# The second feed-forward product with its operands turned round

## The chip, the cores and the metric

One core of one Trainium2 chip. The metric is the device time of one execution in microseconds (us), taken as the median of several runs. Times inside an execution come from one profiled execution and count from the first instruction.

## The reference

One layer of a transformer-like trunk on 512 tokens of width 2048, all in float32: a normalised and modulated input goes through two groups of mixing heads and an output projection (with a residual sum), and then through a gated feed-forward block. The change touches the last product of the last line only:

```python
h = rms_norm(x, norm2_g[layer]) * (1.0 + sc2) + sh2
gate, up = jnp.split(h @ w_ffn_in[layer], 2, axis=-1)
x = x + g2 * ((jax.nn.silu(gate) * up) @ w_ffn_out[layer])
```

The hidden width is 5632 (44 blocks of 128). The output leaves the kernel transposed, as 16 blocks of 128 features by 512 tokens.

## The kernel before, in words

**Three passes.** TensorE multiplies numbers of the type float32r. Each float32 operand is split into a rounded part (`hi`, a ScalarE copy, line 231) and the rest (`lo`, a VectorE subtraction, line 232), and a product is summed from three passes: hi by hi, hi by lo, lo by hi. In all matmuls one operand is stationary (loaded as a block of 128x128) and the other one moves through it; the profile shows the load as PEld and the pass as PE.

**Seven products for eight.** Both feed-forward products are cut into halves in both directions and done with seven block products instead of eight, numbered 1 to 7; sums and differences of the blocks are operands. In the first feed-forward product (lines 1145 to 1191, tiles ffA, ffB, ffC) the loop runs over 42 blocks `f` of hidden features. There the weight block is stationary, and 256 tokens of the activation operands opA to opD move: 7 products of 24 matmuls of 128x256 a block. Two hidden blocks were done before, chunk by chunk, into tiles named ff (lines 985 to 1008), in the same orientation.

**The second product.** Its loop (lines 1267 to 1334) runs over 12 units: six chunks of hidden features (3, 3, 4, 4, 4, 4 steps of 128 of the half width 22), and in each two groups `i` of output columns. A unit does the seven products in the order 2, 1, 7, 6, 4, 5, 3. `multiply` (line 1217) does one product, in pieces of two steps (or one): it splits a 128 x 2 x 512 piece of the weights, then for each of two blocks of 128 tokens takes the activations as the stationary operand and 512 weight columns as the moving one. The accumulators are `A` (two banks, foA), `B` (two for each `i`, foB) and `C` (foC). After a product ScalarE copies the accumulators out (`onto`, line 1239) or VectorE adds them to `O`, which holds tokens in the partitions and 2048 features in the row. The activation operands come by DMA into places in opsA, opsB and opsC.

**The end.** In the two units of the last chunk (units 10 and 11) parts of `O` become final. As the output is wanted with features in the partitions, `emit_out` (line 1252) transposes two 128x128 blocks on TensorE (line 98, with the identity `ident2` stationary) into a half bank that belonged to foB, VectorE multiplies by the gate `G2` and adds the residual (line 1259), and SyncE sends 128x256 numbers out (line 1261). `some_out(3)` puts at most three of those behind each product; what is left comes behind the last one.

**Where the split weights lie.** `ring_pair` (line 211) takes a tile of 2048 + 128 numbers from a ring of three and puts hi and lo at `home[0]` and `home[0] + 1024`; every fourth split goes to a spare place (`spare_here`, later `spare_there`, line 1197). `home[0]` is 48 numbers in the first feed-forward product, with one exception: it is 0 in product 3 of every sixth block (`f % 6 == 4`, line 1178), and it is 0 in all of the second product (line 1202). In the built program before, ring tiles and all moving operands start 32 bytes past a multiple of 256 within a partition, so that the stationary and the moving start differ by 192 bytes modulo 256 with `home[0]` 48, and by 0 with `home[0]` 0. I call that the offset of a pair.

**Order.** A scheduler orders each engine's queue by priorities; splits and copies out carry a raised priority (`AHEAD`).

Of the kernel before, what the change touches and what calls it, by code (L numbers as in the profile page):

```python
# [10 lines left out]
F32 = mybir.dt.float32  # L11
F32R = mybir.dt.float32r
# [5 lines left out]
P = 128  # L18
D = 2048
# [110 lines left out]
def trunk(ctx, tc, a):  # L130
# [79 lines left out]

    def ring_pair(shape, name):
        n = int(np.prod(shape[1:]))
        t = wp.tile([P, 2048 + 128], F32R, tag="pair", name=name)
        out = []
        for b in (home[0], home[0] + 1024):
            v = t[:, b:b + n]
            if len(shape) == 3:
                v = v.rearrange("p (a b) -> p a b", a=shape[1])
            elif len(shape) == 4:
                v = v.rearrange("p (a b c) -> p a b c", a=shape[1], b=shape[2])  # L220
            out.append(v)
        return out
# [42 lines left out]


    hhi = hp.tile([P, KT, T], F32R, tag="hhi", name="hhi")
    hlo = hp.tile([P, KT, T], F32R, tag="hlo", name="hlo")
    xo = xop.tile([P, KT, T], F32, tag="xo", name="xo")
    vctx = ctx.enter_context(ExitStack())  # L270
    vp = vctx.enter_context(tc.tile_pool(name="vp", bufs=1))
# [531 lines left out]


    ohi = hp.tile([P, KT, T], F32R, tag="hhi", name="ohi")
    olo = hp.tile([P, KT, T], F32R, tag="hlo", name="olo")
    last = NH - 1

    def split_o(k):
# [198 lines left out]
                hold(0)  # L1008

    late = hp.tile([P, 2, HALF, 2, HT], F32R, tag="hhi", name="opB")  # L1010
    later = hp.tile([P, 2, HALF, 2, HT], F32R, tag="hlo", name="opC")
    H.update({6: late[:, 0], 7: late[:, 1], 5: later[:, 0], 4: later[:, 1]})
    for j in range(0, HALF, 2):
        V.tensor_sub(block(0, 0, j, 2), block(0, 1, j, 2), block(0, 0, j, 2))
# [55 lines left out]

    yraw = []

    def begin_second():
# [10 lines left out]
        places.append(hp.tile([P, 4, 4, 2, HT], F32R, tag="hlo", name="opsB"))  # L1084
# [107 lines left out]
    tctx.close()  # L1192


    more = places[1][:, 3].rearrange("p n h t -> p (n h t)")

    def spare_there(shape, name):
        n = shape[1] * shape[2]
        return [more[:, i * 1024:i * 1024 + n].rearrange("p (k d) -> p k d", k=shape[1]) for i in range(2)]

    spare[0] = spare_there
    home[0] = 0


    zp = ctx.enter_context(tc.tile_pool(name="zp", bufs=1, side="right", reuse_waits="tile"))
    T2 = []
    ident2 = zp.tile([P, 512], F32, name="ident2")[:, 0:P]
    O = zp.tile([P, 4, D], F32, name="O")
# [8 lines left out]
    def multiply(out, c, q, raw, first, u, sums):  # L1217
        n = CHUNKS[c]
        x = place(7 * c + q)
        for k0 in range(0, n, 2):  # L1220
            w = min(2, n - k0)
            with tc.high_priority(offset=AHEAD):
                for d, e, g in sums:
                    with tc.issue_after(mark[0 if q == 3 and k0 == 0 else 1]):
                        V.tensor_sub(*(t[:, k0:k0 + w] for t in (d, e, g)))
            whi, wlo = split(raw[:, k0:k0 + w], [P, w, T], f"wfo{u}_{q}_{k0}")
            if q == 2:
                mark[k0 > 0] = last_lo[0]
            for j in range(2):
                js = slice(j * P, j * P + P)  # L1230
                for kk in range(w):
                    k = k0 + kk
                    flags = dict(stop=False, skip_group_check=True)
                    PE.matmul(out[j], x[:, k, 0, js], whi[:, kk], start=first and k == 0, **flags)
                    PE.matmul(out[j], x[:, k, 0, js], wlo[:, kk], start=False, **flags)
                    flags["stop"] = k == n - 1
                    PE.matmul(out[j], x[:, k, 1, js], whi[:, kk], start=False, **flags)

    def onto(dst, src, first):
        if first:  # L1240
            with tc.high_priority(offset=2 * AHEAD):
                S.copy(dst, src)
            return
        t = cond[:, taps[0] % 4 * T:taps[0] % 4 * T + T]
        taps[0] += 1
        with tc.high_priority(offset=2 * AHEAD):
            S.copy(t, src)
        V.tensor_add(dst, dst, t)

    slots, turn, outs = [], [0], []  # L1250

    def emit_out(m, th):
        ps = slots[turn[0] % len(slots)]
        turn[0] += 1
        src = O[:, 2 * th:2 * th + 2, m * P:m * P + P]
        for j in range(2):
            PE.transpose(ps[:, j * P:j * P + P], src[:, j], ident2)
        xr = place(7 * (last_c + 1) + m // 4).bitcast(F32).rearrange("p n h t -> p n (h t)")[:, m % 4, th * HT:th * HT + HT]
        V.scalar_tensor_tensor(src, ps.rearrange("p (j t) -> p j t", j=2), mcol(G2, m),
                               xr.rearrange("p (j t) -> p j t", j=2), op0=ALU.mult, op1=ALU.add)  # L1260
        nc.sync.dma_start(a["y"][m][:, th * HT:th * HT + HT].rearrange("p (j t) -> p j t", j=2), src)

    def some_out(n):
        for _ in range(min(n, len(outs))):
# [1 line left out]

    for u, (c, i) in enumerate(units):
        def dst(th, j, dh):
            return O[:, 2 * th + j, dh * 1024 + i * T:dh * 1024 + i * T + T]
# [9 lines left out]
        if u == 2:  # L1279
            nc.sync.dma_start(ident2, a["cst"][:, 0])  # L1280
        y = blocks[u]
        if u == 1:
            T2.append(rp.tile([P, 4, T], F32, tag="forms", name="T2", bufs=1))
        s7 = (T2[0] if u else yraw[0][:, 2])[:, 0:CHUNKS[c]]
        load_y(u + 1, 2)
        load_y(u + 1, 0)
        for q, p in enumerate(ORDER):
            out = {2: B[i], 7: C, 4: C}.get(p, A)
            raw = {2: y[2], 1: y[0], 7: s7, 6: y[1], 4: y[2], 5: y[0], 3: y[3]}[p]
            sums = {6: [(y[0], y[1], y[0]), (y[1], y[3], y[0])], 4: [(y[2], y[2], y[1])]}.get(p, ())  # L1290
            if p == 7:
                with tc.high_priority(offset=AHEAD):
                    for k0 in range(0, CHUNKS[c], 2):
                        ks = slice(k0, min(k0 + 2, CHUNKS[c]))
                        V.tensor_sub(s7[:, ks], y[3][:, ks], y[1][:, ks])
            multiply(out, c, q, raw, p in (1, 7) or p == 2 and first, u, sums)
            if final:
                some_out(3)
            for j in range(2):
                if p == 1:  # L1300
                    onto(dst(0, j, 0), A[j], first)
                    if final:
                        V.tensor_add(dst(0, j, 0), B[i][j], dst(0, j, 0))
                elif p == 7:
                    onto(dst(1, j, 1), C[j], first)
                elif p == 6:
                    onto(dst(1, j, 0), A[j], first)
                elif p == 4:
                    V.tensor_add(dst(1, j, 0), C[j], dst(1, j, 0))
                elif p == 5:  # L1310
                    onto(dst(1, j, 1), A[j], False)
                elif p == 3:
                    if first:
                        S.copy(dst(0, j, 1), A[j])
                    else:
                        V.tensor_add(dst(0, j, 1), A[j], dst(0, j, 1))
            if p == 1:
                ready(0, 0)
                if final:
                    slots += [t[:, h * HT:h * HT + HT] for t in B[i] for h in range(2)]  # L1320
# [12 lines left out]
            if i == 1 and 1 <= q < 4:  # L1333
                load_op(c + 1, q + 3)
# [60 lines left out]
```

## Time and profile before

| | us |
|---|---|
| median of 3 runs | 2238.33 (2236.74 to 2240.53) |
| the profiled execution, its own time | 2237.67 |
| its span, first to last instruction | 2235.9 |
| TensorE matmuls busy | 2203.0 |
| VectorE busy | 1918.1 |
| ScalarE busy | 1160.9 |
| start of the second product (first foB) | 1801.8 |
| first transposition behind the last foA matmul | 2227.35 |

The profiled time exceeds its span by 1.8 us, which lie outside the instructions. A row of the timeline has the start, the length of a run of equal instructions, the engine, the line, output and inputs, the tile's shape and the count; in brackets stands the idle time before it and what ended it. The length of a run of matmuls includes the modelled end of the last one, so a pace is read from start to start.

### The profile page before, as it was taken

The page shows a single profiled execution, that of the slowest core. Times are in us where ns is not written, and L with a number is a line of the kernel's source. Part 1 is how long each engine was busy: PE and PEld are TensorE (multiplying, and loading weights), DVE is VectorE, ACT ScalarE, POOL GpSimd, SP SyncE. Part 2 cuts the span into 40 slices and gives each one's busy share as a digit, 9 for nine tenths or more (in the row PEclk, how much of TensorE's full clock was granted, in tenths as well). Part 3 has the DMA queues.
Part 4 walks back from the last instruction along what each step waited for, and adds up shares of the span by engine and source line. Part 5 has one row for each costly group of instructions (what it writes and reads, how often), then busy time and mean ns, then how long its engine had stood idle before and what let it go on. Part 6 is the DMA issues. An engine that isn't in the chain of part 4 may idle for free.

```text
span 2235.9 us, 35417 instructions
## 1 busy us (share of the span) xinstructions
PE 2203.0 (99%) x14171; PEld 2010.8 (90%) x14171; DVE 1918.1 (86%) x2500; ACT 1160.9 (52%) x1986; POOL 10.1 (0%) x25
## 2 busy tenths in 40 slices
PE   7999999999999999999999999999999999999999
PEld 6899899988888888899999999999999988888887
DVE  8897878899988877698888888888888888988888
ACT  4326665566565632385555555555555555545453
POOL 0000000000000000000000000000000000000000
PEclk9999999999999999999999999999999999999999
DMA  9886536754333288724444444444454486666452
GB/s 369 314 328 243 185 133 225 298 197 153 136 113 113 86 304 337 251 96 170 156 170 156 162 164 144 171 143 169 138 176 147 163 336 251 245 224 234 146 214 68
DMA packets 115264, 437.68 MB, mean 196 GB/s; under 512 B 9854, under 2 KB 58268, under 8 KB 77340
## 3 DMA queue, kind: packets, MB, share of 16 engines
q1 hardware_dynamic: 115100, 435.42, 54.0%
q8 instruction: 111, 1.82, 0.3%
q14 instruction: 53, 0.43, 0.1%
HBM read 386.61 MB, written 48.77 MB: 195 GB/s over the span
## 4 chain that ended last, share of the span: by engine, by line
PE 87%; DVE 8%; ACT 2%; DMA 2%; issue 2%; SPq 0%; DVEq 0%; ACTq 0%
PE ffA L93 20%; PE foA L93 11%; PE ffC L93 10%; PE wo L93 7%; PE foC L93 5%; PE ffB L93 5%; PE sbp L93 4%; PE st L93 4%; PE hgf L93 4%; PE hgg L93 4%; PE hgq L93 4%; PE foB L93 3%; PE ff L93 2%; DVE ada L179 2%; DVE wsb L232 1%
## 5 line engine op out<-in xcount | busy, mean ns | idle before, releaser
L93 PE MATMUL sbp<-wsb,hhi 128*128 128x384 f32 x1024 | 270.1, 343 | 3.0 <-DVE wsb L232 1.8
L179 DVE SCALAR_TENSOR_TENSOR ada<-ada,cond 128x2048 f32<-128x2048 f32 x95 | 217.0, 2287 | 20.3 <-DMA ada<-in_w_ada 20.1
L93 PEld LDWEIGHTS sbp<-wsb,hhi 128*128 128x128 f32 x1024 | 184.2, 189 | 7.5 <-issue 3.3
L93 PE MATMUL sbp<-wsb,hlo 128*128 128x384 f32 x512 | 172.4, 337 | 0.0
L93 PE MATMUL wo<-ohi,wo 128*128 128x512 f32 x480 | 149.3, 391 | 1.3 <-ACT ohi L810 1.3
L93 PEld LDWEIGHTS wo<-ohi,wo 128*128 128x128 f32 x480 | 89.9, 188 | 19.7 <-ACT ohi L810 1.5
L231 ACT CAST wfo<-wfo 128x1024 fp32r<-128x1024 f32 (+1 forms) x72 | 72.6, 1008 | 57.6 <-PE foA L93 51.8
L232 DVE TENSOR_TENSOR wfo<-wfo,wfo 128x1024 fp32r<-128x1024 f32 (+1 forms) x72 | 83.4, 1162 | 20.8 <-ACT wfo L231 20.2
L93 PEld LDWEIGHTS sbp<-wsb,hlo 128*128 128x128 f32 x512 | 96.6, 189 | 0.8 <-issue 0.5
L93 PE MATMUL ffA<-opB,ff 128*128 128x256 f32 x768 | 92.8, 276 | 1.0 <-ACT ff L231 1.0
L93 PE MATMUL ffA<-opD,ff 128*128 128x256 f32 x768 | 93.6, 278 | 0.0
L93 PE MATMUL wo<-olo,wo 128*128 128x512 f32 x240 | 93.4, 390 | 0.0
L93 PE MATMUL ffC<-opC,ff 128*128 128x256 f32 x768 | 92.5, 276 | 0.0
L93 PE MATMUL ffB<-opA,ff 128*128 128x256 f32 x768 | 92.4, 276 | 0.0
L93 PEld LDWEIGHTS ffA<-opB,ff 128*128 128x128 f32 x768 | 89.8, 188 | 1.2 <-ACT ff L231 1.2
L93 PEld LDWEIGHTS ffA<-opD,ff 128*128 128x128 f32 x768 | 90.7, 189 | 0.0
L93 PE MATMUL ffA<-opC,ff 128*128 128x256 f32 x744 | 89.7, 276 | 0.0
L93 PEld LDWEIGHTS ffC<-opC,ff 128*128 128x128 f32 x768 | 89.6, 188 | 0.0
L93 PE MATMUL ffC<-opB,ff 128*128 128x256 f32 x744 | 89.6, 276 | 0.0
L93 PEld LDWEIGHTS ffB<-opA,ff 128*128 128x128 f32 x768 | 89.5, 188 | 0.0
L93 PE MATMUL ffA<-opA,ff 128*128 128x256 f32 x744 | 89.5, 276 | 0.0
L93 PE MATMUL st<-wi,hhi 128*128 128x512 f32 x256 | 75.8, 397 | 11.7 <-ACT hhi L317 11.7
(1003 smaller groups left out, 5884.3 us busy)
## 6 DMA issues: line engine op xcount, KB each, us to landing
ada<-in_w_ada SPq DMA_DIRECT2D x95, 1024.0 KB, 6.4
wfo<-in_w_fo SPq DMA_DIRECT2D x16, 1024.0 KB, 5.0
yraw<-in_w_fo SPq DMA_DIRECT2D x16, 1024.0 KB, 4.9
fix<-in_w_fix SPq DMA_DIRECT2D x14, 1024.0 KB, 5.2
opd<-forms SPq DMA_DIRECT2D x44, 256.0 KB, 2.7
opd<-fhi SPq DMA_DIRECT2D x42, 256.0 KB, 2.7
opsC<-opd SPq DMA_DIRECT2D x10, 1024.0 KB, 6.9
opsA<-opd SPq DMA_DIRECT2D x9, 1024.0 KB, 5.5
```

Of the source, the lines that this page charges most:

```text
L93: self.engine.matmul(out, lhsT, rhs, **kw)
L179: V.scalar_tensor_tensor(w, w, 1.0, row, op0=ALU.mult, op1=ALU.mult, accum_out=col)
L231: S.copy(hi, r)
L232: last_lo[0] = V.tensor_sub(lo, r, hi.bitcast(F32)).ins
```

## The change

In the second product the weight block becomes the stationary operand and 256 tokens of the activations the moving one, as in the first product. A product then has 4 blocks `m` of output features where it had 2 blocks of tokens, and twice as many matmuls of half the width. `O` holds features in the partitions, so the identity and the transpositions go, and line 1263 of the kernel after scales and adds from `O` in SBUF. In the last product of the last unit the sums are done in quarters, each sent out by itself.

```diff
-            for j in range(2):
-                js = slice(j * P, j * P + P)
+            home[0] = 0 if q == 0 and k0 == 0 else 48
...
+            for m in range(4):
+                ms = slice(m * P, m * P + P)
+                half = out[m // 2][:, m % 2 * HT:m % 2 * HT + HT]
                 for kk in range(w):
-                    PE.matmul(out[j], x[:, k, 0, js], whi[:, kk], start=first and k == 0, **flags)
-                    PE.matmul(out[j], x[:, k, 0, js], wlo[:, kk], start=False, **flags)
+                    PE.matmul(half, whi[:, kk, ms], x[:, k, 0], start=first and k == 0 and m % 2 == 0, **flags)
+                    PE.matmul(half, whi[:, kk, ms], x[:, k, 1], start=False, **flags)
-                    PE.matmul(out[j], x[:, k, 1, js], whi[:, kk], start=False, **flags)
+                    PE.matmul(half, wlo[:, kk, ms], x[:, k, 0], start=False, **flags)
...
-        src = O[:, 2 * th:2 * th + 2, m * P:m * P + P]
-        for j in range(2):
-            PE.transpose(ps[:, j * P:j * P + P], src[:, j], ident2)
+        src = O[:, m, th * HT:th * HT + HT]
-        V.scalar_tensor_tensor(src, ps.rearrange("p (j t) -> p j t", j=2), mcol(G2, m),
+        V.scalar_tensor_tensor(src, src, mcol(G2, m), xr, op0=ALU.mult, op1=ALU.add)
...
+            if u == len(units) - 1 and p == 3:
+                for m in range(4):
+                    o = O[:, 12 + m, 0:HT]
+                    V.tensor_add(o, A[m // 2][:, m % 2 * HT:m % 2 * HT + HT], o)
+                    emit_out(12 + m, 0)
+                break
```

The second part moves data. `home[0]` is now 48 in the second product, except in the first piece of each unit, where it is 0. Ring tiles shrink, and the tiles with the tag hlo grow by 32 numbers:

```diff
-        t = wp.tile([P, 2048 + 128], F32R, tag="pair", name=name)
+        t = wp.tile([P, 2048 + 64], F32R, tag="pair", name=name)
...
-    hlo = hp.tile([P, KT, T], F32R, tag="hlo", name="hlo")
+    hlo = hp.tile([P, KT * T + 32], F32R, tag="hlo", name="hlo")[:, 0:KT * T].rearrange("p (k t) -> p k t", k=KT)
...
-    more = places[1][:, 3].rearrange("p n h t -> p (n h t)")
+    more = aside[0][:, 3 * 4 * T + 16:]
...
-    home[0] = 0
```

This moves every tile behind hlo. In the built program after, ring tiles, opB, opC, opsB and opsC still start 32 bytes past a multiple of 256, but opA, opD and opsA 160 bytes past one. The spare place of the second product starts 96 past one. So the offsets (stationary less moving, modulo 256) are: in the first product 192 for opB and opC and 64 for opA and opD; in product 3 of every sixth block, whose moving operand is opD, 128 where it was 0; in the two hidden blocks done before it also 128 where it was 0; in the second product 192 or 64, and in the first piece of each unit 0 or 128.

The transpositions of the end stood in TensorE's queue among the matmuls of the last two units and behind them. TensorE's rows around the last product, before (foA and foB followed by a number are single banks, ident is the identity):

```order
L98 MATMUL foB_18242<-ident_18236,O 128x128 x2
L93 MATMUL foA_18238<-wfo_6_0_21067,opsC 128x512 x4
L93 MATMUL foA_18239<-wfo_6_0_21067,opsC 128x512 x6
L93 MATMUL foA_18238<-wfo_6_2_21082,opsC 128x512 x6
L93 MATMUL foA_18239<-wfo_6_2_21082,opsC 128x512 x6
L98 MATMUL foB_18243<-ident_18236,O 128x128 x2
L98 MATMUL foB_18240<-ident_18236,O 128x128 x2
```

and TensorE's last rows after, where nothing follows the last product:

```order
L93 MATMUL foA_18238<-opsC,wfo_5_0_22781 128x256 x12
L93 MATMUL foA_18239<-opsC,wfo_5_0_22781 128x256 x12
L93 MATMUL foA_18238<-opsC,opsB 128x256 x12
L93 MATMUL foA_18239<-opsC,opsB 128x256 x12
L93 MATMUL foA_18238<-opsC,wfo_6_0_22844 128x256 x12
L93 MATMUL foA_18239<-opsC,wfo_6_0_22844 128x256 x12
L93 MATMUL foA_18238<-opsC,wfo_6_2_22871 128x256 x12
L93 MATMUL foA_18239<-opsC,wfo_6_2_22871 128x256 x12
```

The transpositions, 14 more of which follow those rows before, are gone; the last product now ends with 12 matmuls for each bank of foA.

At the end of each of the first four units (chunks of 3 steps) the scheduler puts the start of the next unit's first product between two products of foA. TensorE before, at the end of the first unit (wfo_5 and wfo_6 are the pieces of the unit's last two products, wfo_0 the first piece of the next unit):

```order
L93 MATMUL foA_18238<-wfo_5_2_18414,opsB 128x512 x3
L93 MATMUL foA_18239<-wfo_5_2_18414,opsB 128x512 x3
L93 MATMUL foB_18242<-wfo_0_0_18459,opsA 128x512
L93 MATMUL foB_18243<-wfo_0_0_18459,opsA 128x512
L93 MATMUL foA_18238<-wfo_6_0_18427,opsB 128x512 x6
```

and the same place after:

```order
L93 MATMUL foA_18238<-opsB,wfo_5_2_18516 128x256 x6
L93 MATMUL foA_18239<-opsB,wfo_5_2_18516 128x256 x6
L93 MATMUL foB_18242<-opsA,wfo_0_0_18585 128x256 x2
L93 MATMUL foA_18238<-opsB,wfo_6_0_18535 128x256 x12
```

Two matmuls of 512 columns between the products have become two of 256. VectorE's last rows after (L1304 adds an accumulator to O, L1263 scales and adds the residual):

```order
L1304 TENSOR_TENSOR O<-foA_18238,O 128x256 x2
L1263 SCALAR_TENSOR_TENSOR O<-O,mod,opsA 128x256 x2
L1304 TENSOR_TENSOR O<-foA_18239,O 128x256 x2
L1263 SCALAR_TENSOR_TENSOR O<-O,mod,opsA 128x256 x2
```

Before, nine rows of line 1259 (one tile of 128x256 each) stood behind the last sum; now two stand behind it, and two between the sums of the two banks.

More of the change, by code (lines that the diff above doesn't have):

```diff
@@ L805, in trunk @@
     ohi = hp.tile([P, KT, T], F32R, tag="hhi", name="ohi")
-    olo = hp.tile([P, KT, T], F32R, tag="hlo", name="olo")
+    olo = hp.tile([P, KT * T + 32], F32R, tag="hlo", name="olo")[:, 0:KT * T].rearrange("p (k t) -> p k t", k=KT)
     last = NH - 1
@@ L1010, in trunk @@
     late = hp.tile([P, 2, HALF, 2, HT], F32R, tag="hhi", name="opB")
-    later = hp.tile([P, 2, HALF, 2, HT], F32R, tag="hlo", name="opC")
+    later = hp.tile([P, KT * T + 32], F32R, tag="hlo", name="opC")[:, 0:KT * T].rearrange("p (s n h t) -> p s n h t", s=2, n=HALF, h=2)
     H.update({6: late[:, 0], 7: late[:, 1], 5: later[:, 0], 4: later[:, 1]})
@@ L1071, in trunk @@
     yraw = []
+    aside = []
     def begin_second():
@@ L1083, in begin_second @@
         load_op(0, 3)
-        places.append(hp.tile([P, 4, 4, 2, HT], F32R, tag="hlo", name="opsB"))
+        aside.append(hp.tile([P, KT * T + 32], F32R, tag="hlo", name="opsB"))
+        places.append(aside[0][:, 0:3 * 4 * T].rearrange("p (q n h t) -> p q n h t", q=3, n=4, h=2))
         for q in range(4, 7):
@@ L1201, in trunk @@
     spare[0] = spare_there
-    home[0] = 0
     zp = ctx.enter_context(tc.tile_pool(name="zp", bufs=1, side="right", reuse_waits="tile"))
     T2 = []
-    ident2 = zp.tile([P, 512], F32, name="ident2")[:, 0:P]
-    O = zp.tile([P, 4, D], F32, name="O")
+    zp.tile([P, 512], F32, name="gap")
+    O = zp.tile([P, KT, T], F32, name="O")
     A = [att(f"foA{j}") for j in range(2)]
@@ L1233, in multiply, with two @@
                     flags = dict(stop=False, skip_group_check=True)
-                    PE.matmul(out[j], x[:, k, 0, js], whi[:, kk], start=first and k == 0, **flags)
-                    PE.matmul(out[j], x[:, k, 0, js], wlo[:, kk], start=False, **flags)
+                    PE.matmul(half, whi[:, kk, ms], x[:, k, 0], start=first and k == 0 and m % 2 == 0, **flags)
+                    PE.matmul(half, whi[:, kk, ms], x[:, k, 1], start=False, **flags)
                     flags["stop"] = k == n - 1
-                    PE.matmul(out[j], x[:, k, 1, js], whi[:, kk], start=False, **flags)
+                    PE.matmul(half, wlo[:, kk, ms], x[:, k, 0], start=False, **flags)
+    def two(src):
+        return src.rearrange("p (m t) -> p m t", m=2)
     def onto(dst, src, first):
+        src = two(src)
         if first:
@@ L1243, in onto @@
             return
-        t = cond[:, taps[0] % 4 * T:taps[0] % 4 * T + T]
+        t = two(cond[:, taps[0] % 4 * T:taps[0] % 4 * T + T])
         taps[0] += 1
@@ L1248, in onto @@
         V.tensor_add(dst, dst, t)
-    slots, turn, outs = [], [0], []
+    outs = []
     def emit_out(m, th):
-        ps = slots[turn[0] % len(slots)]
-        turn[0] += 1
-        src = O[:, 2 * th:2 * th + 2, m * P:m * P + P]
-        for j in range(2):
-            PE.transpose(ps[:, j * P:j * P + P], src[:, j], ident2)
+        src = O[:, m, th * HT:th * HT + HT]
         xr = place(7 * (last_c + 1) + m // 4).bitcast(F32).rearrange("p n h t -> p n (h t)")[:, m % 4, th * HT:th * HT + HT]
-        V.scalar_tensor_tensor(src, ps.rearrange("p (j t) -> p j t", j=2), mcol(G2, m),
-                               xr.rearrange("p (j t) -> p j t", j=2), op0=ALU.mult, op1=ALU.add)
-        nc.sync.dma_start(a["y"][m][:, th * HT:th * HT + HT].rearrange("p (j t) -> p j t", j=2), src)
+        V.scalar_tensor_tensor(src, src, mcol(G2, m), xr, op0=ALU.mult, op1=ALU.add)
+        nc.sync.dma_start(a["y"][m][:, th * HT:th * HT + HT], src)
     def some_out(n):
@@ L1268, in dst @@
         def dst(th, j, dh):
-            return O[:, 2 * th + j, dh * 1024 + i * T:dh * 1024 + i * T + T]
+            m = 8 * dh + 4 * i + 2 * j
+            return O[:, m:m + 2, th * HT:th * HT + HT]
         def ready(th, dh):
@@ L1278, in trunk @@
                 nc.sync.dma_start(place(7 * c + 7 + g).bitcast(F32).rearrange("p n h t -> p n (h t)"), x1d[:, 4 * g:4 * g + 4])
-        if u == 2:
-            nc.sync.dma_start(ident2, a["cst"][:, 0])
         y = blocks[u]
@@ L1297, in trunk @@
             if final:
-                some_out(3)
+                some_out(len(outs) if u == len(units) - 1 and p == 3 else 3)
+            if u == len(units) - 1 and p == 3:
[4 more added lines that the diff above has]
+                break
             for j in range(2):
@@ L1302, in trunk @@
                     if final:
-                        V.tensor_add(dst(0, j, 0), B[i][j], dst(0, j, 0))
+                        V.tensor_add(dst(0, j, 0), two(B[i][j]), dst(0, j, 0))
                 elif p == 7:
@@ L1308, in trunk @@
                 elif p == 4:
-                    V.tensor_add(dst(1, j, 0), C[j], dst(1, j, 0))
+                    V.tensor_add(dst(1, j, 0), two(C[j]), dst(1, j, 0))
                 elif p == 5:
@@ L1313, in trunk @@
                     if first:
-                        S.copy(dst(0, j, 1), A[j])
+                        S.copy(dst(0, j, 1), two(A[j]))
                     else:
-                        V.tensor_add(dst(0, j, 1), A[j], dst(0, j, 1))
+                        V.tensor_add(dst(0, j, 1), two(A[j]), dst(0, j, 1))
             if p == 1:
                 ready(0, 0)
-                if final:
-                    slots += [t[:, h * HT:h * HT + HT] for t in B[i] for h in range(2)]
             elif p in (4, 5, 3):
```

## The prediction

> **What bounds the kernel now.** I read the page first, then the chain of waits in order of time.
>
> ```profile
> PE 2203.0 (99%) x14171; PEld 2010.8 (90%) x14171; DVE 1918.1 (86%) x2500; ACT 1160.9 (52%) x1986; POOL 10.1 (0%) x25
> PE 87%; DVE 8%; ACT 2%; DMA 2%; issue 2%; SPq 0%; DVEq 0%; ACTq 0%
> ```
>
> TensorE is busy all the time and carries 87% of the chain, so only its stream counts, and what follows it at the end. The question is what one matmul costs in either orientation. The chain has both in steady stretches: 48 matmuls of 256 columns (ffA), 24 of 512 (foA, foB).
>
> ```profile
> 1703.88 5.44 PE ffA L93 x48
> ...
> 2107.27 5.44 PE foB L93 x24
> 2112.71 5.44 PE foA L93 x24
> ...
> 2145.35 5.44 PE foB L93 x24
> ```
>
> That is 113.3 ns for 256 columns and 226.7 ns for 512: the same per column. A unit of seven products lasts 2145.35 - 2107.27 = 38.08 us and has no gap. Next, the last two units and the tail as windows; after the matmul clock the last column is GB/s.
>
> ```profile
> 2107.20:2145.20 38.00, 38.00 (x170) 31.46 (x169) 33.01 (x35) 19.05 (x22) 0.00 (x0) 1.00 0.71 263
> 2145.20:2185.30 40.10, 40.10 (x185) 32.72 (x184) 37.37 (x44) 19.05 (x22) 0.00 (x0) 1.00 0.33 112
> 2185.30:2227.35 42.05, 42.05 (x201) 34.24 (x200) 35.78 (x50) 15.98 (x19) 0.00 (x0) 1.00 0.20 54
> 2227.35:2235.90 8.55, 3.32 (x19) 1.83 (x17) 4.41 (x10) 0.00 (x0) 0.00 (x0) 0.75 0.51 138
> ```
>
> The columns of busy time are PE, PEld, DVE, ACT, POOL. Unit 10 takes 40.1 us and unit 11 42.05, and then come 8.55 us without a product. The timeline shows what stands there.
>
> ```profile
> 2178.91 0.60 PE L98 MATMUL foB<-ident,O 128*128 128x128 f32 x4
> 2179.26 0.71 PE L93 MATMUL foA<-wfo,opsC 128*128 128x512 f32 x2
> ...
> 2227.35 2.56 PE L98 MATMUL foB<-ident,O 128*128 128x128 f32 x14
> 2227.55 0.69 DVE L1316 TENSOR_TENSOR O<-foA,O 128x512 f32<-128x512 f32 x1 [0.67 <-PE foA L93]
> 2228.55 3.70 DVE L1259 SCALAR_TENSOR_TENSOR O<-foB,mod,opsA 128x256 f32<-128x256 f32 x8
> 2230.88 0.84 PE L98 MATMUL foB<-ident,O 128*128 128x128 f32 x4 [0.97 <-DVE O L1259]
> ```
>
> **The change part by part.** *Matmuls.* 1848 of 512 columns become 3696 of 256. By the chain's rows 1848 x 226.7 and 3696 x 113.3 are both 418.9 us: no gain, no loss. The Trainium skill ("TensorE: Matmul & The Clock Gate", Back-to-back issue gap) gives an isolated gap of N/2.4 + 2.5 ns, a fixed price per matmul that would cost this change 1848 x 2.5 ns = 4.6 us; the rows disagree, since two matmuls of 256 take exactly one of 512.
>
> *Transpositions, -6.0.* Without them units 10 and 11 last 38.08 us each: 40.10 + 42.05 - 2 x 38.08 = 5.99 us. Nothing is late in their place, as the 35 VectorE instructions of the unit before leave 5 us free; the last units are tighter (a rival below).
>
> *The tail, -2.85.* Before, the last matmul's pace ends at 2227.35, VectorE's last instruction at 2228.55 + 3.70 = 2232.25, and the span 3.65 us later (the last output's transfer and the closing waits). That 3.65 stays. After, VectorE does two sums and two scalings for each bank of foA. Their prices:
>
> ```profile
> L1186 DVE TENSOR_TENSOR up<-ffC,b x42: 412/417/425, 1022.4 to 1799.3; 128x256 f32<-128x256 f32 x42
> L1259 DVE SCALAR_TENSOR_TENSOR O<-foB,mod,opsA x16: 473/478/487, 2187.8 to 2231.8; 128x256 f32<-128x256 f32 x16
> L318 DVE SCALAR_TENSOR_TENSOR hlo<-xo,gain,hhi 128x512 fp32r<-128x512 f32 x16 | 11.9, 746 | 0.0
> L876 DVE SCALAR_TENSOR_TENSOR x<-wo,mod,xr 128x512 f32<-128x512 f32 x15 | 11.1, 749 | 7.8 <-PE wo L93 6.3 <-DMA xr<-in_x 1.5
> ```
>
> L318 reads SBUF alone and L876 a PSUM bank, at the same price, so 0.48 us also holds for the scaling from SBUF. A bank needs 2 x 0.417 + 2 x 0.478 = 1.79 us. The first bank is complete 12 x 113.3 ns = 1.36 us before the end and taken up 0.2 us later (2227.55 against 2227.35), so VectorE ends 1.79 + 1.79 - 1.36 + 0.2 = 2.42 us behind the last matmul; instructions that follow each other overlap a little (eight took 3.70, 0.46 each), so 2.2 at best and 2.0 with more overlap. I take 2.05. Tail: 2.05 + 3.65 = 5.7 for 8.55.
>
> *The offset.* Which addresses does the 113.3 hold for? The first feed-forward product has three paces.
>
> ```profile
> 965.18 3.04 PE L93 MATMUL ff<-opA,wff 128*128 128x256 f32 x24
> 968.06 1.60 PE L93 MATMUL ff<-b,wff 128*128 128x256 f32 x12
> ...
> 1004.40 0.50 PE L93 MATMUL ffA<-opB,ff 128*128 128x256 f32 x2 [0.96 <-ACT ff L231]
> ...
> 1046.93 2.99 PE L93 MATMUL ffC<-opB,ff 128*128 128x256 f32 x24
> 1049.76 2.99 PE L93 MATMUL ffA<-opC,ff 128*128 128x256 f32 x24
> ...
> 1055.41 3.03 PE L93 MATMUL ffA<-opD,ff 128*128 128x256 f32 x24
> 1058.28 2.88 PE L93 MATMUL ffA<-opA,ff 128*128 128x256 f32 x24
> 1061.00 2.88 PE L93 MATMUL ffB<-opA,ff 128*128 128x256 f32 x24
> ```
>
> From start to start, 24 matmuls take 2.88 us at 965 (120 ns each, offset 0), 2.83 at 1047 (117.9, offset 192, after TensorE had stood still at 1004), 2.87 at 1055 (offset 0: block 4, product 3, `home[0]` 0), and 2.72 from 1058 on (113.3, offset 192). So a pair at offset 0 costs 6.7 ns more, a halt leaves a slower pace behind, and one product at offset 0 ends that. The Trainium skill, on the same page (Step-by-step: what each phase is for), says that loading the next weights takes no read bandwidth from the running matmul; by it the addresses would not matter and the +1.9 below would go (2230.1). The rows disagree.
>
> Offsets 64 and 128 occur nowhere before. I take 64 as 192, and 128 as 0: the observed ones lie 64 bytes from, or on, a multiple of 128. Then the first product is unchanged, and the first piece of each unit costs 12 x 24 x 6.7 ns = +1.9 (0 if 128 is harmless and 0 too; 0.97 if 128 alone is, about half of the pieces).
>
> *New waits, +0.8 and +0.5.* ScalarE must have copied a foA bank before product 3 writes it.
>
> ```profile
> 1853.79 1.52 PE L93 MATMUL foA<-opsB 128*128 128x512 f32 x6
> 1855.15 0.67 PE L93 MATMUL foB<-wfo,opsC 128*128 128x512 f32 x2
> 1855.66 4.30 PE L93 MATMUL foA<-wfo,opsB 128*128 128x512 f32 x18
> 1854.94 1.07 ACT L1247 COPY cond<-foA 128x512 f32<-128x512 f32 x2
> ```
>
> Before, two foB matmuls of 0.45 us cover this copy and it is late by 0.06 (1855.66 - 1855.15 - 0.45). After, they cover 0.23, so 0.2 more in each of four units: +0.8 (0 if the copy comes sooner, 1.0 at most). Behind the halt the pace may be 117.9 until the next unit's first piece: 36 matmuls x 4.6 ns = 0.17 in four units, and a little at the start: 0.5 in all, 0 to 1.5.
>
> Sum: -6.0 - 2.85 + 1.9 + 0.8 + 0.5 = -5.65, on the profiled time of 2237.67: **2232.0**. The median of the runs is 0.66 higher. By its bounds the forecast's own range is 2229.5 to 2234. A measurement of this kernel can tell about 0.2% (4.5 us) from no change.
>
> **The rivals.** *Slower: the first product no longer recovers its pace.* Product 3 of block 4 now has offset 128. If that is no conflict, it does not end the slow pace that the halt at 1004 leaves, and no later block does either. Then 1058 to 1802 runs at 2.83 for 2.72: 744 x 0.04 = +30, less 2.6, as the 16 groups of 24 matmuls of the tiles ff (8 chunks, 2 halves of the tokens; offset 128 too) then take 0.16 less each: 2232.0 + 27.4 = 2259. For it: 128 was never seen. Against it: it needs 128 to differ from 0, and the halt to strike as before. It decides at 1058. Chance 0.16.
>
> *Faster: 128 is harmless, and no slow pace is left behind.* The 16 groups save 2.6, seven products 3 save 7 x 0.16 = 1.1, half of the first pieces 0.95: 2227.4 (2225.5 if the stretch 1010 to 1055 is faster as well, 45 x 0.04 = 1.8). Chance 0.13.
>
> *VectorE bounds the last two units.* It was busy 37.37 + 35.78 + 4.41 = 77.6 us there; now it has 2 x 38.08 + 2.05 = 78.2. The rows of its idle time in the last unit speak for it:
>
> ```profile
> 2220.56 0.69 DVE L1248 TENSOR_TENSOR O<-O,cond 128x512 f32<-128x512 f32 x1 [1.73 <-ACT cond L1247]
> 2226.19 0.69 DVE L1316 TENSOR_TENSOR O<-foA,O 128x512 f32<-128x512 f32 x1 [2.79 <-PE foA L93]
> ```
>
> If these 4.5 us stay idle for want of finished sums, VectorE ends 4.5 - 0.6 = 3.9 later: 2235.9. Against it: the scalings no longer wait for transpositions and can fill such holes. Chance 0.10.
>
> *A fixed price per matmul* that the steady rows don't show, because something else hides it there. The rows allow 0.01 us in 48 matmuls; the skill's 2.5 ns would give 2236.6. Chance 0.03.
>
> The forecast has 0.58. The range 2226 to 2239 takes in all but the slower rival (0.84, some of it lost at the edges). Faster: four fifths of the forecast (its edge at 2233 lies inside its range) and the faster rival, 0.60. Slower: that rival and a little, 0.18. The same: 0.22.
>
> **What would show it.** Right: no gap and no line 98 behind unit 9; units of 38.08 + 0.16; 5.7 us from the last foA matmul to the end; 24 matmuls in 2.72 us in foA at offsets 64 and 192 alike and 2.88 in the first foB piece; product 3 of block 4 still at 2.88, with 2.72 behind it. Wrong: 2.83 or more in ffA or ffB behind 1058; PE idle before foA in units 10 and 11, released by VectorE; a second product much longer than 423 us.

## The result, and the profile after

The median of the kernel after is 2259.3 us (2255.91 to 2259.78 in 5 runs), of the kernel before 2238.42 on the same chip; the ratio over all runs is 1.0088, interval 1.0077 to 1.0099. It is slower by 21 us, and the forecast was 6 us faster; 2259.3 lies outside the range of 2226 to 2239. The profiled execution took 2255.91 us, with a span of 2254.1 us for 2235.9 before. Two executions of the experiments below, of 10485 us and of 2745 us (the second at a granted clock of 0.753), are left out of all comparisons.

From the page after, TensorE's row of busy times and the shares of the chain:

```profile
PE 2220.4 (99%) x15955; PEld 2103.2 (93%) x15955; DVE 1919.0 (85%) x2502; ACT 1159.4 (51%) x1986; POOL 10.1 (0%) x25
PE 85%; DVE 9%; DMA 3%; ACT 2%; issue 2%; SPq 0%; DVEq 0%; ACTq 0%
```

TensorE still bounds the kernel and is busy 17 us longer. Two windows tell where. The first is the first feed-forward product from block 5 on (the same matmuls in both kernels), the second everything from the first foB matmul on. Before:

```profile
1058.30:1801.80 743.50, 743.50 (x6555) 743.50 (x6553) 636.15 (x717) 386.31 (x565) 0.00 (x0) 1.00 0.47 161
...
1801.80:2235.90 434.10, 428.87 (x1914) 351.97 (x1912) 377.96 (x433) 215.18 (x269) 0.00 (x0) 0.99 0.57 210
```

and after:

```profile
1059.50:1819.90 760.40, 760.40 (x6554) 760.40 (x6553) 639.08 (x717) 386.02 (x565) 0.00 (x0) 1.00 0.46 158
...
1819.90:2254.10 434.20, 429.62 (x3698) 428.13 (x3697) 376.48 (x435) 214.36 (x269) 0.00 (x0) 1.00 0.58 210
```

The first product, whose code the change does not touch, takes 760.4 - 743.5 = 16.9 us more, with TensorE busy throughout and a granted clock of 1.00 in both. The second product and the tail, which should have been 5.65 shorter, last as long as before. (1.2 us more stand ahead of these windows.)

TensorE's timeline after shows what is slow in the first product. These are product 3 of block 4, block 5 and the start of block 6, one row for a product; rows of split pieces that came out as single matmuls are left out:

```profile
1056.63 3.04 PE L93 MATMUL ffA<-opD,ff 128*128 128x256 f32 x24
1059.51 2.89 PE L93 MATMUL ffA<-opA,ff 128*128 128x256 f32 x24
...
1067.79 2.99 PE L93 MATMUL ffC<-opB,ff 128*128 128x256 f32 x24
1070.61 2.99 PE L93 MATMUL ffA<-opC,ff 128*128 128x256 f32 x24
...
1078.99 2.88 PE L93 MATMUL ffA<-opA,ff 128*128 128x256 f32 x24
1081.71 2.88 PE L93 MATMUL ffB<-opA,ff 128*128 128x256 f32 x24
```

From start to start the products on opA take 2.72 us for 24 matmuls (1078.99 to 1081.71), those on opB and opC 2.82 to 2.83 (1067.79 to 1070.61). Product 3, on opD, takes 2.72 in block 5. Four of seven products in each of 39 blocks are 0.11 slower: 39 x 4 x 0.11 = 17.2, the loss of 16.9 but for rounding. The pace changes where the moving operand passes from a tile that starts 160 bytes past a multiple of 256 (opA, opD) to one that starts 32 past (opB, opC), and changes back on return. Before, all four started at 32.

The second product has the same two starts, in opsA (160) and opsB and opsC (32). Its last two units after:

```profile
2171.09 3.00 PE L93 MATMUL foB<-opsA,wfo 128*128 128x256 f32 x24
...
2193.73 2.99 PE L93 MATMUL foC<-opsB,wfo 128*128 128x256 f32 x24
2196.55 2.88 PE L93 MATMUL foC<-opsB 128*128 128x256 f32 x24
...
2210.15 5.83 PE L93 MATMUL foB<-opsA,wfo 128*128 128x256 f32 x48
...
2243.99 5.60 PE L93 MATMUL foA<-opsC,wfo 128*128 128x256 f32 x48
```

Unit 10 lasts 2210.15 - 2171.09 = 39.06 us and unit 11 about as long (39.28 to the end of the last pace, 2243.99 + 48 x 0.1133 = 2249.43), where 38.24 were forecast; the transpositions are gone, and no engine holds TensorE up, but most of the matmuls run at the slower pace (2.82 from 2193.73 to 2196.55). The tail, by VectorE's last rows:

```profile
2248.27 0.76 DVE L1304 TENSOR_TENSOR O<-foA,O 128x256 f32<-128x256 f32 x2 [1.69 <-PE foA L93]
...
2250.39 0.87 DVE L1263 SCALAR_TENSOR_TENSOR O<-O,mod,opsA 128x256 f32<-128x256 f32 x2
```

VectorE ends at 2251.26, 1.83 behind the last pace, and the span 2.84 later: a tail of 4.7 us, for 8.55 before.

### The profile page after: what moved, and what is told of

Same layout as the page of the kernel before. It is cut to its first block, busy times and chain, and to the rows that moved or that the text cites. A ratio compares the mean times of both kernels' runs of the same rounds, so it can differ in the third digit from the quotient of the medians.

```text
span 2254.1 us, 39013 instructions
## 1 busy us (share of the span) xinstructions
PE 2220.4 (99%) x15955; PEld 2103.2 (93%) x15955; DVE 1919.0 (85%) x2502; ACT 1159.4 (51%) x1986; POOL 10.1 (0%) x25
## 3 DMA queue, kind: packets, MB, share of 16 engines
q8 instruction: 125, 2.05, 0.4%
## 4 chain that ended last, share of the span: by engine, by line
PE 85%; DVE 9%; DMA 3%; ACT 2%; issue 2%; SPq 0%; DVEq 0%; ACTq 0%
PE ffA L93 21%; PE foA L93 11%; PE ffC L93 11%; PE wo L93 7%; PE foC L93 5%; PE ffB L93 5%; PE sbp L93 4%; PE st L93 4%; PE hgq L93 3%; PE hgg L93 3%; PE hgf L93 3%; PE foB L93 3%; DVE ada L179 2%; PE ff L93 2%; DMA ada<-in_w_ada 1%
## 5 line engine op out<-in xcount | busy, mean ns | idle before, releaser
L93 PEld LDWEIGHTS ffA<-opC,ff 128*128 128x128 f32 x744 | 89.7, 188 | 0.2 <-ACT b L1047 0.2
L93 PEld LDWEIGHTS ffC<-opB,ff 128*128 128x128 f32 x744 | 89.8, 188 | 0.0
```

The costliest lines, as they stand in the source:

```text
L93: self.engine.matmul(out, lhsT, rhs, **kw)
```

## The experiments

At first there were three theories. A, the starts: a change between moving operands whose starts lie 128 bytes apart leaves the slower pace. B, the reset: product 3 at offset 128 no longer ends a slow pace, which was the forecast's slower rival. C: the turned second product is itself the loss. The runs of one group were made together on one chip, with runs of the kernel before among them; where no range is given, a time is that of a single execution.

**One start for all moving operands.** The four tiles with the tag hlo grow by 64 numbers, not 32, so that opA, opD and opsA too start at 32 bytes. All else is as in the change.

```diff
-    hlo = hp.tile([P, KT * T + 32], F32R, tag="hlo", name="hlo")...
+    hlo = hp.tile([P, KT * T + 64], F32R, tag="hlo", name="hlo")...
```

> The tiles with the tag hlo grow by 64 numbers instead of 32, so that every moving operand again starts 32 bytes past a multiple of 256; everything else is as in the kernel after. Theory A (a switch between moving operands whose starts differ by 128 bytes leaves the slower pace): no switch is left, 24 matmuls take 2.72 us in all products of the first feed-forward product behind block 4, the stage shortens by about 18 us, and the sum of the prediction holds at last, 2232 +- 3. Theory B (product 3 of every sixth block no longer ends a slow pace, because its offset is 128): here its offset is 0 again, so the first product recovers too, 2232 to 2240. Theory C (the turned second product is itself the loss): 2250 to 2259.

Median 2235.24 us (2232.62 to 2237.52 in 10 runs) against 2236.94 before, ratio 0.999 (0.998 to 1.0). The kernel was run once more for its profile.

> The kernel of e1_one_class once more, for an undisturbed profile. Theory A: 24 matmuls in 2.72 us in all products behind block 4 of the first feed-forward product; seven products at 2.88; in the second product the first piece of each unit at 2.88, and slow stretches only behind halts; about 2235.

2235.3 us. Its windows from block 5 on and from the first foB on:

```profile
1060.00:1803.50 743.50, 743.50 (x6554) 743.50 (x6553) 635.98 (x717) 386.06 (x565) 0.00 (x0) 1.00 0.47 162
...
1803.50:2233.50 430.00, 425.37 (x3698) 423.86 (x3696) 376.74 (x435) 214.44 (x269) 0.00 (x0) 1.00 0.57 212
```

The first product is back at 743.5 to the tenth, and the second part is 4.2 us shorter than in the change (430.0 against 434.2). Adding 128 bytes of padding takes away the whole loss, so C falls. A and B both fit, as product 3 of every sixth block has offset 0 again here; the runs below part them. The turning round is a gain in its own part, 4.1 us in this profile (434.1 to 430.0). By the medians of the whole kernel 1.7 us of it are left, and the interval of the ratio does not rule out no change.

**The addresses alone.** The kernel before, not turned, with the smaller ring tile and the 32 numbers behind hlo alone.

```diff
-        t = wp.tile([P, 2048 + 128], F32R, tag="pair", name=name)
+        t = wp.tile([P, 2048 + 64], F32R, tag="pair", name=name)
-    hlo = hp.tile([P, KT, T], F32R, tag="hlo", name="hlo")
+    hlo = hp.tile([P, KT * T + 32], F32R, tag="hlo", name="hlo")[:, 0:KT * T]...
```

> The kernel before with the two changed tile sizes alone (ring tiles of 2048 + 64, hlo longer by 32 numbers), nothing turned round. Theory A: blocks of the first feed-forward product lose 4 of 7 products x 24 x 4.4 ns = 0.42 us each, 40 blocks make +17, 2255. Theory B: +17 to +30, all products slow behind block 4. Theory C: no change, 2238.

Median 2258.6 us (2258.02 to 2260.0 in three runs) against 2236.94, ratio 1.0095 (1.0078 to 1.0112): the whole loss without any turning. The window from block 5 on and, from the second product (weights move, 512 wide), matmuls with stationary opsA at offset 128:

```profile
1058.60:1819.00 760.40, 760.40 (x6554) 760.40 (x6554) 639.37 (x718) 386.06 (x565) 0.00 (x0) 1.00 0.45 158
```

```profile
2154.52 2.95 PE L93 MATMUL foA<-wfo,opsA 128*128 128x512 f32 x12
2157.31 2.95 PE L93 MATMUL foA<-opsB,opsA 128*128 128x512 f32 x12
```

The first product shows the same 760.4 as the change. The rest sits in the second product, 3.7 us longer than before, where 12 matmuls with a stationary block at offset 128 take 2.79 us instead of the 2.72 of before.

**Product 3 of every sixth block at offset 0 again**, in the change.

```diff
-        home[0] = 48 if aside else 0
+        home[0] = 48 if aside else 32
```

> The kernel after, with home[0] 32 numbers instead of 0 in product 3 of every sixth block of the first feed-forward product, so that this one product has the offset 0 that it had in the kernel before (its moving operand starts 160 bytes past a multiple of 256). Theory A: no change, products 6, 7, 5 and 4 of each block still take 2.83 us and the others 2.72; 2256 to 2260. Theory B: with the offset 0 the pace recovers in block 4 and stays, the stage shortens by 18 us; about 2240.

2261.03 us. The timeline from that product of block 4 on:

```profile
1059.79 3.02 PE L93 MATMUL ffA<-opD,ff 128*128 128x256 f32 x24
1062.65 2.99 PE L93 MATMUL ffA<-opA,ff 128*128 128x256 f32 x24
...
1085.06 2.88 PE L93 MATMUL ffB<-opA,ff 128*128 128x256 f32 x24
1087.78 2.99 PE L93 MATMUL ffA<-opB,ff 128*128 128x256 f32 x24
```

The pattern stays, 2.72 on opA and 2.83 on opB, and here opA is slow as well (2.83) in the block behind each of the seven products at offset 0. B falls as the cause of this loss, and A is left.

**No pair at offset 0.** The kernel with one start, with `home[0]` 48 everywhere (offsets 192, and 64 in spare places).

```diff
-        home[0] = 48 if aside else 0
+        home[0] = 48
...
-            home[0] = 0 if q == 0 and k0 == 0 else 48
+            home[0] = 48
```

> As e1_one_class, with home[0] 48 everywhere in both feed-forward products: no product at offset 0 is left. If a halt leaves a slow pace and only a product at offset 0 ends it, 24 matmuls take 2.83 us from about 1010 to the end of the first product (+30 less seven products at 0.16: +29 against e1_one_class) and in the second product (about +16): 2275. If offset 192 settles by itself: as e1_one_class less 3, about 2229.

2230.87 us in this one execution, 742.6 us in the stage from block 5 on. What this number is worth came out only later, below.

**Offsets 64 and 192 in turn, one start.** As the last, with `home[0]` 16 in products 1, 2 and 3. The moving operands keep one start, the stationary ones alternate.

```diff
-        home[0] = 48
+        home[0] = 16 if name[-2:] in ("_1", "_2", "_3") else 48
```

> The reverse: the kernel of e4_no_zero_offset, in which all moving operands start 32 bytes past a multiple of 256, with home[0] 16 in products 1, 2 and 3 of the first feed-forward product and 48 in the others, so that the offset changes between 64 and 192 twice a block. If the moving operand's start decides: all products at 2.72, about 2231. If the change of the offset decides: slow products again, +17, about 2248.

2230.32 us. The window from block 5 on:

```profile
1058.20:1800.80 742.60, 742.60 (x6554) 742.60 (x6554) 636.21 (x718) 386.10 (x565) 0.00 (x0) 1.00 0.47 162
```

The window holds 39 blocks of 168 matmuls; that is 742.6 / 6552 = 113.3 ns for each of them in this execution, at 64 (opA, opD) and at 192 (opB, opC), through every change between the two. So neither an offset of 64 nor the change of offset costs anything while the moving start stays the same.

**One offset, two starts.** The counterpart in the change: the starts stay 160 and 32, and `home[0]` is chosen so that all seven products have offset 192.

```diff
-        home[0] = 48 if aside else 0
+        home[0] = 16 if name[-2:] in ("_1", "_2", "_3") else 48
...
-        off = 0 if home[0] else 80
+        off = 0 if home[0] == 48 else 32
```

> The kernel after, its addresses unchanged (opA and opD start 160, opB and opC 32 bytes past a multiple of 256), but home[0] is 16 in products 1, 2 and 3 of the first feed-forward product, whose moving operands are opA and opD, and 48 in the others, so that the offset is 192 in all seven (the exception of every sixth block is dropped). If the switch between moving operands that start 128 bytes apart leaves the slow pace: products 6, 7, 5 and 4 stay at 2.83 us, about 2258. If the change of the offset between 64 and 192 leaves it: all products at 2.72, the stage 18 us shorter, about 2240.

2268.23 us: 2.83 in every block of the first product, on opA too, longer than either theory said. This did not tell A from something else, since TensorE had stood still at about 1012 us, came out of it at 2.83, and nothing in the first product of this kernel ends such a pace. So the reset was added:

```diff
-        home[0] = 16 if name[-2:] in ("_1", "_2", "_3") else 48
+        home[0] = (16 if aside else 32) if name[-2:] in ("_1", "_2", "_3") else 48
```

> This is the kernel with offset 192 for all seven products on the split starts (160 and 32), which took 2268.2 us with 117.9 ns in the whole first product, plus one thing: product 3 of every sixth block at offset 0 again. Theory 'a pace that persists' (the halt at 1013 us left 117.9 and nothing ended it; where moving and stationary start move together the pace is kept): 2.72 us for 24 matmuls in all products from 1060 us on, opB and opC included; 744 us x 0.04 = 30 us less, 1 more for the seven products at offset 0: about 2239. Theory 'the moving start alone' (each change between starts 160 and 32 costs the pace, whatever the stationary start): 2.83 in opB and opC as in the change, 2.72 in opA and opD: about 18 less than 2268, 2251. Rival 'offset 192 at start 160 is slow by itself': unchanged, 2268.

2265.98 us, close to the 2268 of the rival in that text. The timeline behind the reset:

```profile
1056.77 3.04 PE L93 MATMUL ffA<-opD,ff 128*128 128x256 f32 x24
1059.64 2.88 PE L93 MATMUL ffA<-opA,ff 128*128 128x256 f32 x24
1062.36 2.88 PE L93 MATMUL ffB<-opA,ff 128*128 128x256 f32 x24
...
1067.91 2.99 PE L93 MATMUL ffC<-opB,ff 128*128 128x256 f32 x24
...
1079.22 2.99 PE L93 MATMUL ffA<-opA,ff 128*128 128x256 f32 x24
1082.05 2.99 PE L93 MATMUL ffB<-opA,ff 128*128 128x256 f32 x24
```

The rival's time, but not by its cause: behind the product at offset 0 opA runs at 2.72, with start 160 and offset 192. The first change of start from 160 to 32 loses that pace, behind each of the seven such products. The change back does not win it back here; in the kernel after it does, where the offset goes from 192 to 64 with it. So the change from 160 to 32 loses the pace at a constant offset too, and what a return does also depends on the stationary start. The theory that the pace is kept where both starts move together falls.

**Starts on a multiple of 256.** The kernel without a pair at offset 0, with 56 numbers of padding ahead of everything, so that all moving operands start at 0 and the offsets stay.

```diff
+    const.tile([P, 56], F32, name="shim")
...
-        off = 0 if home[0] else 80
+        off = 56 if home[0] else 80
```

> The kernel of e4_no_zero_offset with 224 bytes of padding ahead of its tiles, so that the moving operands start on a multiple of 256 bytes instead of 32 past one; the offsets stay (192 or 64 in the feed-forward products, 0 in the rest). From the rows before, matmuls at offset 0 take 120.0 ns for 256 columns and 226.7 for 512, which is 0.417 ns a column and 13.3 ns beside; at offset 192 6.7 ns beside. If only the offset counts: no change, 2231. If the fixed part comes from the 32 bytes by which the operands miss a multiple of 64: it shrinks, 24 matmuls of 256 columns in 2.56 us in the first product, 0.06 of 800 us = 47 us there and some 25 us in the second, so 2160 or less.

2260.96 us, 30 more than without the padding, which neither theory said. Then the same with product 3 of every sixth block at offset 0:

```diff
-        home[0] = 48
+        home[0] = 48 if aside else 0
...
-        off = 56 if home[0] else 80
+        off = 56 if home[0] else 8
```

> This is the kernel whose operands start at a multiple of 256 bytes, which took 2261.0 us with 117.9 ns per matmul from 1013 us to 1834 us, plus product 3 of every sixth block at offset 0. Theory 'a pace that persists': the first such product, at about 1060 us, ends the slow pace, and the rest of the first product takes 2.72 us per 24: 2261.0 - 30 + 1 = 2232. Rival 'a start at a multiple of 256 is slow by itself': unchanged, 2261 to 2262.

2232.55 us. Its timeline around the reset:

```profile
1015.05 2.99 PE L93 MATMUL ffC<-opC,ff 128*128 128x256 f32 x24
1017.88 2.99 PE L93 MATMUL ffA<-opD,ff 128*128 128x256 f32 x24
...
1060.32 2.88 PE L93 MATMUL ffA<-opA,ff 128*128 128x256 f32 x24
1063.04 2.88 PE L93 MATMUL ffB<-opA,ff 128*128 128x256 f32 x24
```

2.83 behind the halt at 1012 us (1015.05 to 1017.88), and 2.72 (1060.32 to 1063.04) behind the one product at offset 0, which stands just ahead of the third row. So a start on a multiple of 256 is not slow by itself, and the reset is worth 28 us here. Was the fast pace without any reset then luck? The kernel without a pair at offset 0 was timed again, unchanged:

> The one-class kernel without any piece at offset 0, as looked at before (2230.87 us, 113.3 ns behind the halt at 1011 us), timed. Theory 'the pace behind a halt comes out the same in each execution of a program': all runs within 2229 to 2233, about 6 us below the kernel before. Rival 'it is chance in each execution': some runs near 2260, since nothing here ends a slow pace in the first product.

2261.98 us (2260.38 to 2265.49 in 5 runs), ratio 1.0104 (1.0091 to 1.0117). The same program had given 2230.87, in one execution on another chip. The first execution's rows behind the halt and its stage:

```profile
1014.25 2.88 PE L93 MATMUL ffC<-opC,ff 128*128 128x256 f32 x24
1016.97 2.88 PE L93 MATMUL ffA<-opD,ff 128*128 128x256 f32 x24
```

```profile
1057.70:1800.30 742.60, 742.60 (x6555) 742.60 (x6554) 636.55 (x718) 386.16 (x565) 0.00 (x0) 1.00 0.47 162
```

and the later one's:

```profile
1013.50 3.10 PE L93 MATMUL ffA<-opC,ff 128*128 128x256 f32 x24
1016.43 2.99 PE L93 MATMUL ffC<-opC,ff 128*128 128x256 f32 x24
```

```profile
1061.60:1833.30 771.70, 771.70 (x6554) 771.70 (x6554) 641.07 (x718) 386.17 (x565) 0.00 (x0) 1.00 0.45 156
```

One program, one clock, and 2.72 or 2.83 behind the halt. Nothing in the first product ends the slower pace here, which costs 771.7 - 742.6 = 29.1 us. It ends at the start of the second product, without any pair at offset 0 (the moving operand stands first in a row; opsB as the stationary one is the spare place, at offset 64):

```profile
1833.34 2.99 PE L93 MATMUL foB<-opsA,wfo 128*128 128x256 f32 x24
1836.16 1.54 PE L93 MATMUL foB<-opsA,opsB 128*128 128x256 f32 x12
1837.54 4.24 PE L93 MATMUL foA<-opsA,wfo 128*128 128x256 f32 x36
```

24 matmuls at offset 192 take 2.82 us; behind 12 at offset 64, 36 at offset 192 take 4.08 (to 1841.62), 113.3 ns each. In both profiles of this program every slow pace in the second product ends so, at the first or second piece at offset 64: a reset needs no offset 0.

**The copies covered.** Against the halts themselves, in the kernel without a pair at offset 0: the pieces of a chunk of three steps become one and two steps (they were two and one), and the weight cast of the next unit's second piece is put behind ScalarE's copies of product 5.

```diff
-        for k0 in range(0, n, 2):
-            w = min(2, n - k0)
+        for k0 in ((0, 1) if n == 3 else (0, 2)):
+            w = 1 if n == 3 and k0 == 0 else 2
...
-            whi, wlo = split(raw[:, k0:k0 + w], [P, w, T], f"wfo{u}_{q}_{k0}")
+            whi, wlo = split(raw[:, k0:k0 + w], [P, w, T], f"wfo{u}_{q}_{k0}", done[0] if q == 0 and k0 else None)
```

> The same with the seven waits of TensorE for ScalarE's copies covered: in units of three steps the piece of one step goes first and that of two last, and the weight cast for the next unit's second piece stands behind the copies of product 5. Left out of TensorE's stream: seven halts of 0.25 to 0.3 us and the stretches at 117.9 behind them (5.7, 11, 7 us in units 1 to 3, 17 us each in units 5, 7 and 9: together 75 us x 0.04 = 3.0). Theory 'the halts cost, and leave the slow pace': 2230.9 - 2.0 - 3.0 = 2226. Rival 'the halts only move' (the cast of the next piece is late in their place): 2230 to 2231.

Twelve runs in two groups: 2227.87 to 2230.82 in four, 2258.23 to 2261.79 in eight (median 2258.9). In the kernel without this edit, the last product of unit 5 in TensorE's rows and then ScalarE's:

```profile
1987.49 6.06 PE L93 MATMUL foA<-opsC,wfo 128*128 128x256 f32 x48
...
1986.33 0.59 ACT L1255 COPY cond<-foA 128x512 f32<-128x512 f32 x1 [0.31 <-PE foA L93]
1987.58 1.05 ACT L231 CAST opsB<-wfo 128x1024 fp32r<-128x1024 f32 x1 [0.66 <-PE foA L93]
1988.53 0.58 ACT L1255 COPY cond<-foA 128x512 f32<-128x512 f32 x1
```

and with it:

```profile
2018.26 5.60 PE L93 MATMUL foA<-opsC,wfo 128*128 128x256 f32 x48
...
2018.46 0.59 ACT L1259 COPY cond<-foA 128x512 f32<-128x512 f32 x1 [0.77 <-PE foA L93]
2018.94 1.05 ACT L235 CAST opsB<-wfo 128x1024 fp32r<-128x1024 f32 x1
```

A cast of 1.05 us stood ahead of the second copy; behind it instead, 48 matmuls take 5.60 for 6.06. So the halts of units 5, 7 and 9 are gone (the profile is of an execution of the slower group). Those at the ends of units 0 to 3 are not (two matmuls of 272 and 222 ns at each), and one that waits for VectorE's sums has come in their place at 1923 us (0.7 us). The rival was half right: most of the expected 5 us did not come, and neither theory had the second group.

**Covered, and with the reset.** The two groups can come from what a halt leaves, or from something that lasts the whole run. This kernel adds product 3 of every sixth block at offset 0.

```diff
-        home[0] = 48
+        home[0] = 48 if aside else 0
```

> The kernel with the copies covered, whose times fell into two groups (2227.9 to 2230.8 us in 4 runs, 2258.2 to 2261.8 in 8), plus product 3 of every sixth block at offset 0. Theory 'a halt leaves 113.3 or 117.9 ns by chance, and a product at offset 0 ends the slower pace': the two groups become one; each run has at worst 117.9 from 1013 to 1058 us (+1.8) and seven products at offset 0 (+1.1): all runs within 2228 to 2233, median about 2231. Rival 'the second group is something else that lasts the whole run': still two groups some 30 us apart.

2233.03 us (2230.55 to 2237.03 in 10 runs) against 2238.81, ratio 0.9975 (0.9966 to 0.9985): one group, so the second theory falls. Five of the ten lie above the 2233 that was expected at most. This kernel is the one that is faster than before, by 0.25%. Its last units and the two windows:

```profile
2153.46 2.88 PE L93 MATMUL foB<-opsA,wfo 128*128 128x256 f32 x24
...
2191.54 5.60 PE L93 MATMUL foB<-opsA,wfo 128*128 128x256 f32 x48
...
2224.18 5.60 PE L93 MATMUL foA<-opsC,wfo 128*128 128x256 f32 x48
```

```profile
1063.60:1807.20 743.60, 743.60 (x6555) 743.60 (x6554) 635.67 (x718) 385.68 (x565) 0.00 (x0) 1.00 0.47 161
...
1807.20:2234.30 427.10, 421.65 (x3698) 420.30 (x3696) 378.36 (x435) 216.59 (x269) 0.00 (x0) 1.00 0.58 214
```

Units 10 and 11 last 38.08 us each (2191.54 - 2153.46, and 2224.18 + 5.44 - 2191.54). The second part takes 427.1 for 434.1.

## Why the prediction was wrong

The failed step is in the part on the offset: "I take 64 as 192, and 128 as 0 ... Then the first product is unchanged." As to the offsets it was right for the first product: with one moving start, 64 and 192 both run at 2.72, and product 3 of block 4 at offset 128 takes 2.88 (1056.63 to 1059.51), as at 0. But the same edit also put opA, opD and opsA on another start than opB, opC, opsB and opsC. The front part lists those starts, and I used them only to work out differences between stationary and moving operand. All rows of the two products before have one moving start (the transpositions aside, in which the identity moves and the blocks of O are stationary, the other way round than the front part says), so nothing in them could show what a second one does, and the bound on this unknown was made from offsets alone. The term of 0 measured 16.9 us, and the addresses alone, without the turning, give the whole loss. By the profiles the miss is 2255.9 - 2232.0 = 23.9 us: 16.9 in the first product, 4.2 in the second that one start gives back (434.2 to 430.0), 1.5 in waits and paces there (5.65 - 4.1), and 1.2 ahead of both.

The other steps:

- *Matmuls, no gain, no loss:* right. With one start 48 matmuls of 256 columns take 5.44 us, as 24 of 512 did.
- *Transpositions, -6.0:* right, shown where the slower pace is absent (38.08 us in both of the last units of the kernel with copies covered and reset). VectorE held nothing up there.
- *Tail, -2.85:* measured -3.85. VectorE's 2.05 came out as 1.83, and the 3.65 behind it as 2.84; why that is shorter was not tested.
- *First pieces, +1.9:* about right. The records of the first pieces in the kernel with one start show 119 to 120 ns; 288 x 6.5 ns = 1.9.
- *Waits and the pace behind them, +0.8 and +0.5:* too small. The copies cost a halt at the ends of units 0 to 3, as forecast, and also in units 5, 7 and 9, where the cast stood ahead of a copy, which the ScalarE queue of after would have shown. In the kernel with one start 19 matmuls lose 2.2 us by halts, and some 520 more, not counting first pieces, run at 117.9 (520 x 4.6 ns = 2.4); 0.7 us of such losses stood in the second product before. So -6.0 - 3.85 + 1.9 + 2.2 + 2.4 - 0.7 = -4.05, near the measured 4.1 and short of 5.65. The step that failed here: the first pieces at offset 0 were to end the slower pace, and most of the 520 stand behind such a piece. Where a piece at offset 192 follows it, the pace is 113.3 (six units of six); where one at offset 64 follows, it is 118 (five of six), even behind a fast stretch.
- *The slower rival:* its time, 2259, is the one measured, but for another reason. Its condition, that offset 128 does not end a slow pace, is not settled. In the kernel with the addresses alone opA runs at 2.83 in blocks 3 and 4, and at 2.72 behind product 3 of block 4, at offset 128. But in the change the faster pace is back already in product 3 of block 3 (1037.16 to 1039.89, 2.73 us), at offset 64. The rival's mechanism exists all the same: where no such product is left, a slow pace lasts through the first product and costs 29.1 us, for the 30 that the forecast gave it. A time that fits is no proof of its cause: the rows behind 1059 differ (2.72 and 2.83 in turn for the one, 2.83 throughout for the other).

I wrote that the rows disagree with what the Trainium skill says ("TensorE: Matmul & The Clock Gate", Step-by-step: what each phase is for), that loading the next weights takes no read bandwidth from the running matmul. That was more than the rows can say. The runs do not show which reads meet, or whether any do; they show that the same stage at the same granted clock takes 743.5 or 760.4 us depending on start addresses, which that sentence does not account for.

Still open is why any of this is so: why a change from 160 to 32 loses the pace, why a step of the offset from 192 to 64 wins it back and one from 0 to 64 mostly loses it, and what in a halt decides between 2.72 and 2.83. Starts other than 0, 32 and 160 were not tried for the moving operands.

## What to carry to other kernels

List the start of every moving and every stationary operand modulo 256 bytes before and after a change of layout, and treat each value, and each change between values in TensorE's stream, as unmeasured until a row shows it. When padding moves one tile, ask what lies behind it: here 128 bytes behind hlo cost 17 us in a stage that the change never touched, and 128 more gave them back. And before trusting one fast execution, look for a halt behind which nothing resets the pace: one program gave 2230.87 and 2261.98 us.

## What the runs showed of the hardware that I had not expected

- The pace of TensorE has a memory. 24 matmuls of 256 columns take 2.72 or 2.83 us at the same addresses and a granted clock of 1.00, and the value lasts for hundreds of microseconds (742.6 against 771.7 us for one program).
- Behind a halt of TensorE it is one or the other by chance, in executions of one program on one chip: four runs of twelve near 2229 us, eight near 2259. A reset of the pace added, ten runs of ten lie between 2230.55 and 2237.03.
- A product at offset 0 (2.87 us) ended the slower pace in the first product of all four kernels with one moving start whose profiles show it (2.83 ahead, 2.72 behind). What comes next counts: with two starts it did so where offset 192 followed, and not where 64 followed.
- Offset 0 is not needed. Pieces at offset 64 between others at offset 192 ended a slower pace that had lasted from 1013 to 1836 us.
- A change of the moving operand's start by 128 bytes, from 160 to 32, costs the fast pace (2.72 to 2.83 in each of 39 blocks). Changes of the stationary start by 128 bytes, between offsets 64 and 192, do not (742.6 us for the stage). A stationary operand at offset 128 has its own price: 12 matmuls of 512 columns took 2.79 us for 2.72.
